# Allocating 640 bytes of small tables ahead of a 52 KB tile ring, in an encoder layer kernel

## The chip, the cores and the metric

The kernel runs on one core of a Trainium2 chip. The metric is device time in microseconds (us), the median of several executions; lower is better. One further execution was taken with the hardware profiler, and every row shown here is from it.

## The reference

One layer of a bidirectional encoder is applied to two batches, 512 tokens ("s") and 256 tokens ("p"), of width 1024, in float32:

```
xn = RMSNorm(x)
[qA|kA|vA|qB|kB|vB] = xn @ w_in                 # w_in: 1024 x 2304
oA = dilated sliding-window attention, 8 heads, three dilations merged
oB = windowed attention (+-128 tokens) with a sink logit, 8 query heads, 2 key heads
h  = x + concat(RMSNorm(oA), RMSNorm(oB)) @ w_o # 1024 x 1024
y  = h + relu(RMSNorm(h) @ w_up)^2 @ w_down     # 1024 x 4096, 4096 x 1024
```

## The kernel before

Float32 products are made from three matmuls: each operand is split into a high part and a low part (both float32r), and high x high, high x low and low x high are summed in PSUM. `mm3(out, xh, xl, wh, wl, ...)` issues the three, on lines 213, 214 and 215; in the projections and in the down product the x part is the stationary operand (loaded with a weight load) and the weight part is the moving operand, 512 columns. `product` with `mm` (lines 682 to 694) does the same for w_up, with the w_up part stationary and 384 columns of x moving. In the profile a matmul is named out<-moving,stationary.

Tiles come from pools. A pool gives each tag its own stretch of each partition, in the order in which the first tile of the tag is asked for; tiles of one tag share its buffers in turn. The pool `sb` lives through the whole kernel, `att` until the attention and both output projections are issued, and `mlp` takes the place of `att` after that. The tag "heap" in `sb`, called the ring here, has `NHEAP = 13` buffers of 4,096 bytes per partition. It holds in turn, among others:

- the raw weights of the first two projections (`wis0_*r`, `wis1_*r`), half of the queries and keys of batch s, the queries and keys of batch p, the transposed x of batch p (`xTp`), most transposed probabilities (`PTs`), the mixed heads of batch p (`mxp`);
- the normalised rows ahead of their transpose (`hs`), the raw and split parts of w_up (`wu..r`, `wu..a`, `wu..b`, `wu..c`, `wu..h`, `wu..l`) and of w_down (`wd..r`, `wd..h`, `wd..l`).

It does not hold: the x of batch s (`xTs`), the values of batch s (`vAs`), the mixed heads of batch s (`mxs`), the activations `u` and the MLP's input `hn`, which lie in the tag "big"; one low part of w_up, `wul`, one block of `hn` and the keys `kBs`, which lie in the tag "b12"; the split weights of the projections (`wis_*`, `wip_*`, `wos_*`, `wop_*`), most of their raw loads, and the probabilities before the transpose (`prs`), which lie in `att`; the four sums `T` and one block `wu..d`, which lie in `mlp`; the identity matrix `ident`, which is the moving operand of every transpose.

These are the addresses in bytes per partition that the program of before is built with. The pool begins behind 4,096 bytes of scratch and four constants of 32 bytes each.

| what | first byte | remainder by 256 |
|---|---|---|
| ring "heap", 13 x 4,096 | 4,224 | 128 |
| `ident`, 512 | 57,472 | 128 |
| `mhalf`, `rx`, `ones`, `gat`, 32 each | 57,984 to 58,111 | 128, 160, 192, 224 |
| tag "big", 5 x 12,288 | 74,496 | 0 |
| tag "b12", 12,288 | 136,384 | 192 |
| split weights in `att`, 6 x 4,096 | 169,472 | 0 |
| raw weights in `att`, 2 x 4,096 | 208,384 | 0 |
| `prs` in `att`, 6 x 2,048 | 216,576 | 0 |
| `T` in `mlp`, 4 x 12,288 | 169,536 | 64 |
| `wu..d` in `mlp` | 206,400 | 64 |

Within a tile, the slices that the matmuls take start at further multiples of 512 bytes, so an operand has the remainder of its tile.

The order of the work is the order of the program text, arranged by the generators `fills`, `pace` and `attend` from written-out costs, and by the tile scheduler; none of it reads an address. The MLP runs as 16 passes over pairs of w_up and w_down blocks. From pass 2 on, `up(i)` makes seven products of 12 matmuls (lines 683; blocks A00, S2, S1, A01, S4, S3, A11) and `down(i)` 72 matmuls (6 token tiles x 2 halves x 2 blocks x 3). `down(i)` is interleaved with `up(i+1)` for its first token tile and runs by itself after that, except for `down(0)` and the last.

Of the kernel before, what the change touches and what calls it, by code (L numbers as in the profile page):

```python
# [8 lines left out]
F32 = mybir.dt.float32  # L9
# [5 lines left out]
P = 128  # L15
# [25 lines left out]
def tile_encoder(ctx: ExitStack, tc: tile.TileContext, a):  # L41
# [5 lines left out]
    sb = ctx.enter_context(tc.tile_pool(name="sb", bufs=1))  # L47
# [5 lines left out]
    def heap(shape, dt, name):  # L53
        return sb.tile(shape, dt, tag="heap", name=name, bufs=NHEAP)
# [6 lines left out]
        return ps.tile([P, 512], F32, tag="ps", name=name, bufs=8)  # L61

    zero = heap([P, 512], mybir.dt.bfloat16, "zero")
    nc.vector.memset(zero, 0.0)
    warm = acc("warm")
    for _ in range(WARM):
        nc.tensor.matmul(warm, zero[:, :P], zero, start=True, stop=True)
    ident = sb.tile([P, P], F32, name="ident")  # L70
    make_identity(nc, ident)
    mhalf = sb.tile([P, 8], F32, name="mhalf")
    nc.gpsimd.memset(mhalf, -0.5)
    rx = sb.tile([P, 6], F32, name="rx")
    ones = sb.tile([P, 1], F32, name="ones")
    nc.vector.memset(ones, 1.0)
    gat = sb.tile([P, 8], F32, name="gat")
    nc.scalar.dma_start(gat, a["gat"])
    nc.scalar.activation(rx[:, 0:1], ones, AF.Exp)

# [956 lines left out]
```

## Time before, and how to read its profile

| | us |
|---|---|
| median of 3 executions | 901.11 (899.32 to 901.6) |
| the profiled execution, its own time | 899.42 |
| its span, first to last instruction | 897.6 |
| TensorE busy in the span | 883.7 |

The profile names engines PE (TensorE matmul), PEld (TensorE weight load), DVE (VectorE), ACT (ScalarE), POOL (GpSimd) and SP (SyncE, which issues DMAs). L215 is line 215 of the kernel. A matmul's listed duration includes its time in the pipeline, so consecutive matmuls overlap in it; the pace of TensorE is read from the distance between the starts of matmuls that follow each other. In the chain of waits a run of pieces of one engine, each starting where the last ended, gives these starts directly.

### The profile page before, as it was taken

Reading aid. Unit: us, or ns where it says so; the run is one execution under the profiler, and the core shown is the slowest. Engines: PE = TensorE matmul, PEld = TensorE weight load, DVE = VectorE, ACT = ScalarE, POOL = GpSimd, SP = SyncE. Lnnn points to the kernel's source line nnn. Section 1 sums busy time; section 2 is a strip of 40 time slices with the busy share of each in tenths; the row PEclk is TensorE's granted clock in tenths of the full one; section 3 lists DMA queues with packets and bytes.
Section 4 is the critical chain, followed back from the end, with each engine's and each line's share of the span. In section 5 each row is a group of like instructions: output and inputs, shape, how many; then the busy total and the mean of one; then the engine's idle time right before and its main releaser. Section 6 shows DMA issues by size and latency. Waiting matters only on the chain.

```text
span 897.6 us, 12569 instructions
## 1 busy us (share of the span) xinstructions
PE 883.7 (98%) x4740; PEld 762.7 (85%) x4740; DVE 627.8 (70%) x1134; ACT 401.7 (45%) x795; POOL 232.2 (26%) x252
## 2 busy tenths in 40 slices
PE   9999999999999999899999999999999999999998
PEld 6877888877878788798889988988998898899886
DVE  7666778887898756959777557657755765775654
ACT  6466578777777644735323222322322232232210
POOL 0412645481254100502511220221122022112000
PEclk9999999999999999999999999999999999999999
DMA  9121111321125115304122112112211211121103
GB/s 367 45 93 49 50 46 48 118 71 63 57 78 188 65 48 191 114 1 141 50 92 94 41 54 94 49 70 71 94 43 53 95 49 68 71 95 42 53 1 140
DMA packets 22252, 72.92 MB, mean 81 GB/s; under 512 B 2480, under 2 KB 2992, under 8 KB 22192
## 3 DMA queue, kind: packets, MB, share of 16 engines
q1 hardware_dynamic: 22048, 72.12, 22.8%
q8 instruction: 37, 0.61, 0.3%
q14 instruction: 23, 0.19, 0.1%
q10 hardware_dynamic: 144, 0.00, 0.0%
HBM read 68.97 MB, written 3.15 MB: 80 GB/s over the span
## 4 chain that ended last, share of the span: by engine, by line
PE 88%; DVE 6%; ACT 3%; issue 1%; DMA 1%; POOL 1%; SPq 0%; ACTq 0%
PE pjs L213 4%; PE pjs L215 4%; PE pjs L214 4%; PE u L683 3%; PE wos L213 2%; PE scsA L425 2%; PE wos L215 2%; PE wos L214 2%; PE pjp L213 2%; PE ptsA L479 1%; PE pjp L215 1%; PE pjp L214 1%; PE posA L497 1%; PE scsB L425 1%; DVE hs L641 1%
## 5 line engine op out<-in xcount | busy, mean ns | idle before, releaser
L798 POOL TENSOR_TENSOR s<-s,s 128x384 f32<-128x384 f32 x14 | 15.0, 1070 | 70.3 <-ACT s L790 70.3
L436 ACT ACTIVATE prsA<-prsA,NM 128x512 f32<-128x512 f32 x32 | 23.1, 724 | 18.1 <-DVE NM L432 18.0
L704 ACT ACTIVATE u<-s 128x384 fp32r<-128x384 f32 x28 | 14.7, 524 | 27.6 <-DVE s L782 26.9
L432 DVE CUSTOM_DVE_ANT_0 prsA<-scsA,MA 128x512 f32<-128x512 f32 x32 | 21.5, 683 | 6.5 <-PE scsA L425 6.4
L704 ACT ACTIVATE u<-r 128x384 fp32r<-128x384 f32 x22 | 11.6, 528 | 31.7 <-DVE r L793 19.4
L432 DVE CUSTOM_DVE_ANT_0 prsB<-scsB,MB,cst 128x256 f32<-128x256 f32 (+1 forms) x32 | 16.8, 542 | 5.4 <-PE scsB L425 3.3
L436 ACT ACTIVATE prsB<-prsB,NM 128x256 f32<-128x256 f32 (+1 forms) x32 | 17.7, 556 | 5.4 <-DVE NM L432 4.0
L479 PE MATMUL ptsA<-ident,prsA 128*128 128x128 f32 x128 | 17.4, 273 | 1.2 <-ACT xTp1h L201 1.2
L213 PE MATMUL pjs<-wis_0hi,xTs 128*128 128x512 f32 (+1 forms) x48 | 17.8, 393 | 0.1
L213 PE MATMUL pjs<-wis_1hi,xTs 128*128 128x512 f32 (+1 forms) x48 | 17.5, 375 | 0.0
L479 PEld LDWEIGHTS ptsA<-ident,prsA 128*128 128x128 f32 x128 | 14.8, 140 | 3.1 <-ACT xTp1h L201 1.4
L214 PE MATMUL pjs<-wis_1lo,xTs 128*128 128x512 f32 (+1 forms) x48 | 17.2, 359 | 0.0
L215 PE MATMUL pjs<-wis_1hi,xTs 128*128 128x512 f32 (+1 forms) x48 | 17.1, 357 | 0.0
L214 PE MATMUL pjs<-wis_0lo,xTs 128*128 128x512 f32 (+1 forms) x48 | 16.6, 356 | 0.0
L215 PE MATMUL pjs<-wis_0hi,xTs 128*128 128x512 f32 (+1 forms) x48 | 16.5, 355 | 0.0
L782 DVE SCALAR_TENSOR_TENSOR s<-s 128x384 f32<-128x384 f32 x28 | 15.4, 551 | 0.0
L705 DVE TENSOR_TENSOR u<-s,u 128x384 fp32r<-128x384 f32 x28 | 15.4, 550 | 0.0
L673 PE MATMUL hT<-ident,hs 128*128 128x128 f32 x96 | 12.2, 273 | 3.1 <-ACT wop_1hi L149 2.3
L673 PEld LDWEIGHTS hT<-ident,hs 128*128 128x128 f32 x96 | 10.9, 140 | 4.4 <-ACT wop_1hi L149 2.7
L705 DVE TENSOR_TENSOR u<-r,u 128x384 fp32r<-128x384 f32 x22 | 13.1, 599 | 1.9 <-ACT u L704 1.8
L213 PEld LDWEIGHTS pjs<-wis_0hi,xTs 128*128 128x128 f32 x48 | 9.4, 199 | 4.1 <-ACT xTs L201 1.0
L215 PE MATMUL pjs<-wis_2hi,xTs 128*128 128x512 f32 x32 | 12.8, 400 | 0.0
(1540 smaller groups left out, 3254.6 us busy)
## 6 DMA issues: line engine op xcount, KB each, us to landing
wis_1r<-w_in SPq DMA_DIRECT2D x5, 512.0 KB, 5.7
wip_0r<-w_in SPq DMA_DIRECT2D x5, 512.0 KB, 3.1
wip_1r<-w_in SPq DMA_DIRECT2D x5, 512.0 KB, 3.2
wis_2r<-w_in SPq DMA_DIRECT2D x4, 512.0 KB, 5.7
wis_3r<-w_in SPq DMA_DIRECT2D x4, 512.0 KB, 6.0
wis_0r<-w_in SPq DMA_DIRECT2D x4, 512.0 KB, 5.8
wip_2r<-w_in SPq DMA_DIRECT2D x4, 512.0 KB, 3.2
wip_3r<-w_in SPq DMA_DIRECT2D x4, 512.0 KB, 3.1
```

What stands on the lines that cost most here:

```text
L213: gated(nc.tensor.matmul(out, xh, wh, start=start, stop=False))
L214: nc.tensor.matmul(out, xh, wl, start=False, stop=False)
L215: nc.tensor.matmul(out, xl, wh, start=False, stop=stop)
L425: last[0] = nc.tensor.matmul(sc[j][:, :w], q[x][pr, qt * P:(qt + 1) * P], k[y][pr, k0 * P:k1 * P], start=(x + y == 0), stop=(x == 1))
L432: nc.vector.tensor_tensor_reduce(tt[:, :w], sc[j][:, :w], mask(qt, k0, w), scale=1.0, scalar=BIG if sink is None else sink[:, h - 8:h - 7] ...
L436: nc.scalar.activation(tt[:, :w], tt[:, :w], AF.Exp, bias=nm_ap, scale=-1.0, accum_out=LS[:, b.t0 + qt, h:h + 1])
L479: last[0] = nc.tensor.transpose(pt[:, n * P:(n + 1) * P], tts[j][:, n * P:(n + 1) * P], ident)
L673: tr = nc.tensor.transpose(pt[:, i * P:(i + 1) * P], hs[:, i * P:(i + 1) * P], ident)
L683: i = nc.tensor.matmul(out, w, x, start=start, stop=stop, skip_group_check=True)
L704: nc.scalar.activation(u[:, 0, us], r, AF.Copy)
L705: nc.vector.tensor_sub(u[:, 1, us], r, u[:, 0, us].bitcast(F32))
L782: nc.vector.scalar_tensor_tensor(c, c, 0.0, c, op0=ALU.max, op1=ALU.mult)
```

## The change

The five `sb.tile` calls of the small tables `ident`, `mhalf`, `rx`, `ones` and `gat` are moved up, ahead of the first tile of the ring. No instruction is added, removed or moved.

```
+    ident = sb.tile([P, P], F32, name="ident")
+    mhalf = sb.tile([P, 8], F32, name="mhalf")
+    rx = sb.tile([P, 6], F32, name="rx")
+    ones = sb.tile([P, 1], F32, name="ones")
+    gat = sb.tile([P, 8], F32, name="gat")
 
     zero = heap([P, 512], mybir.dt.bfloat16, "zero")
     nc.vector.memset(zero, 0.0)
     warm = acc("warm")
     for _ in range(WARM):
         nc.tensor.matmul(warm, zero[:, :P], zero, start=True, stop=True)
-    ident = sb.tile([P, P], F32, name="ident")
     make_identity(nc, ident)
-    mhalf = sb.tile([P, 8], F32, name="mhalf")
     nc.gpsimd.memset(mhalf, -0.5)
-    rx = sb.tile([P, 6], F32, name="rx")
-    ones = sb.tile([P, 1], F32, name="ones")
     nc.vector.memset(ones, 1.0)
-    gat = sb.tile([P, 8], F32, name="gat")
     nc.scalar.dma_start(gat, a["gat"])
     nc.scalar.activation(rx[:, 0:1], ones, AF.Exp)
```

The tables take 512 + 4 x 32 = 640 bytes.

## Rows read from the trace of the kernel before

**Rows 1.** Page: busy time and share of each engine; PE and clock in 40 slices

```profile
PE 883.7 (98%) x4740; PEld 762.7 (85%) x4740; DVE 627.8 (70%) x1134; ACT 401.7 (45%) x795; POOL 232.2 (26%) x252
...
PE   9999999999999999899999999999999999999998
...
PEclk9999999999999999999999999999999999999999
```

**Rows 2.** Busy time by stretch: window, length, engines with instructions, clock, DMA share, GB/s

```profile
0.00:25.00 25.00, 23.72 (x94) 17.70 (x95) 18.73 (x32) 16.75 (x21) 0.92 (x9) 1.00 0.93 368
...
150.00:300.00 150.00, 144.62 (x934) 119.27 (x933) 125.89 (x308) 114.00 (x290) 63.59 (x84) 0.99 0.26 89
300.00:450.00 150.00, 146.06 (x813) 127.86 (x812) 111.66 (x189) 74.44 (x150) 39.33 (x35) 1.00 0.26 91
450.00:540.00 90.00, 90.00 (x449) 80.89 (x448) 58.60 (x88) 26.87 (x38) 17.71 (x15) 1.00 0.19 66
...
700.00:800.00 100.00, 100.00 (x500) 90.21 (x499) 66.01 (x99) 28.92 (x42) 18.37 (x15) 1.00 0.20 69
```

**Rows 3.** Chain of waits, 580 to 600 us: start, length, what (62 pieces of `down(5)`)

```profile
580.35 0.23 PE y5s L214
580.57 0.23 PE y5s L215
...
581.96 0.24 PE y5s L215
...
583.59 0.24 PE y5s L213
...
585.21 0.24 PE y5s L214
...
594.51 0.23 PE y5p L215
594.74 2.11 PE u7a L683 x12
```

**Rows 4.** Chain of waits, 9 to 28 us: the first projection, 24 matmuls between rows

```profile
11.31 0.91 PE pjs L213 x4
...
16.75 0.91 PE pjs L213 x4
...
22.19 0.91 PE pjs L213 x4
...
27.63 0.45 PE xss L240 x5
```

**Rows 5.** Chain of waits, 336 to 350 us: output projection of batch s

```profile
339.46 0.23 PE wos L215
...
341.55 0.23 PE wos L215
...
346.32 0.23 PE wos L215
346.55 0.44 PE mxp L592 x4
```

**Rows 6.** TensorE in order of time, 349.5 to 366 us: output projection of batch p

```profile
349.77 0.39 PE L214 MATMUL wop<-wop_0lo,mxp 128*128 128x512 f32 x1
...
357.90 0.63 PE L213 MATMUL wop<-wop_3hi,mxp 128*128 128x512 f32 x2
...
363.25 0.40 PE L215 MATMUL wop<-wop_0hi,mxp 128*128 128x512 f32 x1
365.96 0.30 PE L673 MATMUL hT<-ident,hs 128*128 128x128 f32 x1 [2.31 <-ACT wop_1hi L149]
```

**Rows 7.** Chain of waits, 379 to 401 us: first w_up products, both w_up parts in the ring

```profile
379.35 12.50 PE u L683 x71
391.85 1.75 PE hT L673 x16
```

**Rows 8.** Chain of waits, 500 to 518 us: the products of `up(4)`

```profile
500.48 2.11 PE u4a L683 x12
502.59 2.09 PE u4b L683 x12
504.68 2.09 PE u4c L683 x12
506.77 2.12 PE u4a L683 x12
508.88 2.09 PE u4b L683 x12
...
511.91 2.12 PE u4c L683 x12
...
515.40 2.11 PE u4b L683 x12
```

**Rows 9.** Chain of waits, 84 to 90 us: 256 columns, moving in the ring

```profile
85.97 1.90 PE posA L497 x16
```

**Rows 10.** Chain of waits, 137 to 142.5 us: 256 columns, no operand in the ring

```profile
137.24 0.12 PE pjs L214
...
139.16 0.12 PE pjs L215
```

**Rows 11.** Groups by shape: splits of 1024-column weights on ACT and DVE

```profile
L149 ACT ACTIVATE wos_3hi<-wos_3r 128x1024 fp32r<-128x1024 f32 x2 | 2.1, 1062 | 1.4 <-PE wos L215 1.4
...
L149 ACT ACTIVATE wd10h<-wd10r 128x1024 fp32r<-128x1024 f32 x1 | 1.1, 1062 | 0.1
...
L153 DVE TENSOR_TENSOR wos_0lo<-wos_0r,wos_0hi 128x1024 fp32r<-128x1024 f32 x2 | 2.5, 1226 | 2.6 <-ACT wos_0hi L149 2.1 <-PE ptpA L469 0.5
...
L153 DVE TENSOR_TENSOR wd12l<-wd12r,wd12h 128x1024 fp32r<-128x1024 f32 x1 | 1.2, 1226 | 0.2 <-ACT wd12h L149 0.2
```

**Rows 12.** DMA issues: size of one, median us from issue to landing

```profile
wos_1r<-w_o SPq DMA_DIRECT2D x2, 512.0 KB, 3.2
...
wd22r<-w_down SPq DMA_DIRECT2D x1, 512.0 KB, 3.2
```

**Rows 13.** Groups by shape: transposes

```profile
L479 PE MATMUL ptsA<-ident,prsA 128*128 128x128 f32 x128 | 17.4, 273 | 1.2 <-ACT xTp1h L201 1.2
...
L673 PE MATMUL hT<-ident,hs 128*128 128x128 f32 x96 | 12.2, 273 | 3.1 <-ACT wop_1hi L149 2.3 <-DVE hs L666 0.5 <-DVE hs L665 0.3
```

**Rows 14.** Groups of the first 12 us: the first split

```profile
L151 DVE CAST wis_0hi<-wis_0r 128x512 fp32r<-128x512 f32 x1 | 0.4, 426 | 3.2 <-DMA wis_0r<-w_in 3.2
```

## The prediction

> **What bounds the kernel now.** I read the page first: TensorE is busy 98% of the span, its clock row shows the full level (2.4 GHz) in every slice, VectorE is at 70% [rows 1]. Then the stretches: from 450 us on TensorE is busy 100% of each window while no other engine passes 66%, and even the two attention and output-projection stretches are at 96 and 97% [rows 2]. So time can only be won or lost in how fast TensorE steps from one matmul to the next, and in the MLP each nanosecond of that step is a nanosecond of the result. The chain of waits shows the step, because its pieces follow each other start to start.
>
> **The step depends on where the operands lie.** Take five runs of 512-column matmuls, all at the full clock.
>
> - First projection, moving in `att` (remainder 0 by 256), stationary in "big" (0): 27.63 - 11.31 = 16.32 us for 72 matmuls, 226.7 ns each [rows 4].
> - Output projection of batch s, same two places: after other work the first nine take 341.55 - 339.46 = 2.09 us, 232 ns each, then 21 take 346.32 - 341.55 = 4.77 us, 227 ns each [rows 5].
> - Output projection of batch p, same code and the same buffers for the moving operand, stationary in the ring (128): 357.90 - 349.77 = 8.13 us for 35, 232.3 ns each, and it never settles [rows 6].
> - Down product, moving in the ring (128), stationary in "big" (0): 594.74 - 580.35 = 14.39 us for 62, 232.1 ns each; every seventh step is a 0.24 (581.96, 583.59, 585.21), to the end of the run [rows 3].
>
> So a run whose two operands have the same remainder settles, after some nine matmuls, at 226.7 ns; one whose remainders differ by 128 stays at 232.1 to 232.3. Two of the runs differ from the others only in which operand is the odd one. The excess is 5.4 ns, 2.4%.
>
> **What the change does, part by part.** It issues nothing new and moves no instruction; the tables keep the same 640 bytes. The ring moves up by 640 bytes, from 4,224 to 4,864 = 19 x 256, remainder 0; all that lies behind the tables stays; `ident` goes to 4,224, which is again remainder 128.
>
> 1. *Down product.* 16 passes x 72 = 1,152 matmuls; moving goes from 128 to 0, stationary stays at 0, the pair of the first projection. In the 14 interleaved passes a run of 62 is unbroken [rows 3]; less nine to settle, 53 x 5.4 ns = 0.286 us, x 14 = 4.0 us. The two other passes: 63 x 5.4 ns x 2 = 0.7 us. The ten matmuls of a pass that stand between products I leave at 232 ns. Gain 4.7 us; bounds 0 and 1,152 x 5.4 ns = 6.2 us.
> 2. *First w_up products.* 192 matmuls of 384 columns, three quarters of them with `hn` in "big" (0) and both w_up parts in the ring: 12.50 us for 71, 176.1 ns [rows 7]. No row has this shape settled; between 226.7 ns at 512 columns and 16 steps in 139.16 - 137.24 = 1.92 us, 120.0 ns, at 256 [rows 10], the line gives 173.3 ns, an estimate. The long run gives 62 x 2.8 ns = 0.17 us, the short ones as much again in all. Gain 0.3 us; bounds 0 and 0.5.
> 3. *Products of `up`.* With `hn`: 14 x 36 = 504, at 2.11 or 2.12 us for 12, 176.4 ns; with `T` and a ring block: 504, at 2.09 for 12, 174.2 ns [rows 8]. Each third weight load is `wul` at 192, which stays. For `hn` the ring loads then agree and `wul` does not: between 173.3 and 176.4 ns, so 0 to 1.6 us gained. For `T` (64) the differences from its loads go from 192 and 128 to 64 and 128, which are those that `hn` has now at 176.4 ns: 0 to 1.1 us lost. I take half of each: they nearly cancel, 0.
> 4. *Projections of batch p.* 192 matmuls with `xTp` and 96 with `mxp` as stationary would agree. The first kind comes in short runs between attention steps, too short to settle; after the run of the second kind TensorE idles 2.31 us for a weight split [rows 6], which takes up what it wins. 0; bound 288 x 5.5 ns = 1.6 us gained.
> 5. *Probabilities times values.* 128 matmuls of 256 columns with `PTs` as moving operand and "big" as stationary, some 190 with those of the other kinds: 1.90 us for 16, 118.8 ns [rows 9], against 120.0 where both agree [rows 10]. At this width agreeing is the slower: loss 190 x 1.2 ns = 0.2 us.
> 6. *Transposes.* `ident` and `hs` agree before (128 and 128) and not after; `prs` (0) does not agree before. Both last 273 ns [rows 13]: 0.
> 7. *Other engines.* The split of a 1,024-column weight takes 1,062 ns on ScalarE and 1,226 on VectorE whether its tiles are at 0 (`wos`) or at 128 (`wd`) [rows 11]: 0. Were it not, both lie beside TensorE's full stretches.
> 8. *Loads.* 512 KB land in 3.2 us at 0 and at 128 [rows 12]: 0. The one load waited for at the start costs 3.2 us of VectorE [rows 14]. The Trainium skill (DMA: Bandwidth & Descriptors, How a descriptor splits into AXI transactions) says that a descriptor off a 256-byte boundary starts at the boundary below and pays for the unused beats; for a 4,096-byte row at 128 that is 132 beats for 128, an estimate, 3% of a load. The two landing times here show none of it, and by the rule the start would win 0.1 us.
>
> Sum: -4.7 - 0.3 + 0.2 = -4.8 us. The profiled execution took 899.42 us, 897.6 of span and 1.8 around it that the change does not touch: it would take 894.6. It lies 1.7 us below the median of the three; on the median, 901.1 - 4.8 = 896.3 us, 0.5% less. A measurement of this kernel can tell 0.3%, 2.7 us, from no change.
>
> **Rivals.**
>
> *The remainder is not the cause (no change).* The operands of the slow runs lie in the ring, at low addresses, and those of the fast runs do not; the place, or something else in which those runs differ, could set the step, and the ring stays where it is but for 640 bytes. Against it: the nine slow steps ahead of the settled ones in the same run [rows 5] look like two streams that fall into step, which a place alone would not give. Then 901.1 us, within 0.3%. The Trainium skill speaks for this rival: TensorE: Matmul & The Clock Gate, Part 2: What happens when you issue a matmul, gives TensorE two independent SBUF read ports, one for the streamed operand and one for the weights, so that their addresses could not matter. The two paces of one shape at one clock, 226.7 and 232.1 ns, do not agree with that being all.
>
> *Every pair that agrees gains at once.* No nine to settle, the short runs too: the upper bounds of 1, 3 and 4 without the loss for `T`: 6.2 + 0.5 + 1.6 + 1.6 = 9.9 us, 891.2. Against it: rows 5 show the slow start.
>
> *Slower: agreeing too well.* By 512, `att` has remainder 0 and "big" 256, and so do the settled runs; the moved ring has 256, the same as "big". A pair equal by 512 stands in the trace only as `wu..d` with `T` (64 and 64): 2.11 us for 12, the last piece of the group, against 2.09 for the other `T` products, 1.7 ns more each [rows 8]. If the down product did likewise instead of settling, it would lose 1,152 x 1.7 ns = 1.9 us; if each step were as its slowest now, 0.24 us, 9.1 us. I take the middle: 1,152 x 4 ns = 4.6 us, 905.7. It decides once the down step passes 232.1 + 2.3 = 234.4 ns. Against it: that group is cut by a change of neighbours, which alone slows the first nine.
>
> **How the numbers follow.** Forecast 0.66, with its own range of 894.3 to 898.4 (the down product between the settled gain and half of it); no change 0.18; gains at once 0.09; slower 0.07. The time given is the forecast's, 896.3. The range takes in the no-change case up to the highest of the runs shown and some of the larger gain: 892.5 to 901.7. Faster by over 0.3%: the forecast and the larger gain, less a little for a half-sized gain, 0.74; within 0.3%: 0.19; slower: 0.07.
>
> **What would show it.** In the profile after: the run of 62 down matmuls takes about 9 x 232 + 53 x 226.7 ns = 14.1 us instead of 14.39, with no 0.24 behind its ninth; the 71 first w_up products 12.3 instead of 12.50; three passes, 500.48 to 594.74 before (94.3 us), take 93.4. Step 5 shows as 16 `posA` in 1.92, step 6 as 273 ns unchanged, steps 7 and 8 as the same 1,062, 1,226 and 3.2. The prediction is wrong if the down run keeps its seven-step pattern, or settles at a pace other than 226.7, or if `T` products rise above 176.4.

## The result and the profile after

The changed kernel took 892.76 us (median of 4, 892.65 to 894.54) beside 900.84 of the kernel before (4 runs, 899.32 to 901.6): ratio 0.9917, interval 0.9899 to 0.9935. Timed again in five rounds it took 893.67 (6 runs, 892.79 to 894.86) beside 900.42 (11 runs, 899.12 to 904.7): ratio 0.9923, interval 0.9904 to 0.9943. By the medians that is 8.1 us less at first and 6.75 the second time, and the interval of the second leaves 5.1 to 8.6; 4.8 were forecast. The 6.75 us are used below. Of the two profiled executions, 892.82 and 899.42 us, the difference is 6.6.

The page after: the same instructions, shares within a point and the same clock row as in [rows 1]. TensorE's busy time falls from 883.7 to 877.5 us, and GpSimd's from 232.2 to 229.1.

```profile
span 891.0 us, 12569 instructions
...
PE 877.5 (98%) x4740; PEld 761.9 (86%) x4740; DVE 628.6 (71%) x1134; ACT 402.0 (45%) x795; POOL 229.1 (26%) x252
...
PEclk9999999999999999999999999999999999999999
```

By stretch, the columns being those of [rows 2]: TensorE was full in both MLP windows before and is full now, so its busy time can show nothing there. What changes is how many matmuls fit: 456 for 449, and 503 for 500. The windows cut the passes at other places than before, and a pass mixes two widths, so the sign of these counts says more than their size.

```profile
450.00:540.00 90.00, 90.00 (x456) 81.89 (x455) 59.49 (x88) 27.36 (x39) 18.30 (x15) 1.00 0.20 69
700.00:800.00 100.00, 100.00 (x503) 90.64 (x502) 67.10 (x101) 29.96 (x43) 18.30 (x15) 1.00 0.21 73
```

The chain of waits after, in the run of 62 down matmuls that answers to [rows 3]:

```profile
578.21 0.23 PE y5s L214
...
579.81 0.23 PE y5s L215
...
592.28 2.09 PE u7a L683 x12
```

592.28 - 578.21 = 14.07 us, 226.9 ns each, against 14.39 and 232.1 before. The first seven take 579.81 - 578.21 = 1.60 us, 0.01 more than seven steps of 226.7 ns: room for two or three slow ones. The other 55 take 12.47, 226.7 each. No piece of the run has 0.24, where before every seventh had. The three passes from the first product of `up(4)` (below) to that of `up(7)` take 592.28 - 499.28 = 93.0 us, where 93.4 were forecast for 94.3.

The same view for the first w_up products [rows 7], for the products of `up(4)` [rows 8], and for 16 `posA` [rows 9]:

```profile
379.49 12.33 PE u L683 x71
```

```profile
499.28 2.09 PE u4a L683 x12
501.37 2.10 PE u4b L683 x12
503.46 2.11 PE u4c L683 x12
505.57 2.10 PE u4a L683 x12
507.67 2.08 PE u4b L683 x12
...
510.67 2.08 PE u4c L683 x12
...
514.13 2.08 PE u4b L683 x12
```

```profile
85.97 1.91 PE posA L497 x16
```

The seven pieces add up to 14.64 us for 84 matmuls, against 14.73 before. One pass, from the first product of `up(3)` to that of `up(4)`, takes 499.28 - 468.28 = 31.00 us, before 500.48 - 469.06 = 31.42: 0.32 of the 0.42 us come from the down run and 0.09 from the products. The starts of `up(2)` and `up(3)`, before and after:

```profile
437.68 2.11 PE u2a L683 x12
...
469.06 2.11 PE u3a L683 x12
```

```profile
437.25 2.09 PE u2a L683 x12
...
468.28 2.09 PE u3a L683 x12
```

**Where the time went.** The chain over the whole span is cut at the first product of `up(2)`, the start of the steady MLP. It starts at 437.25 us after and at 437.68 before. From there to the end of the span it is 891.0 - 437.25 = 453.75 us after and 897.6 - 437.68 = 459.9 before. So the attention stretches and the first pass give 0.4 us, and the steady MLP 6.15. Fourteen passes at 0.42 us are about 5.9 of it; the rest comes behind the last full pass.

### The profile page after: what moved, and what is told of

The parts are those of the page before. It is cut to its first block, busy times and chain, and to the rows that moved or that the text cites. A ratio compares the mean times of both kernels' runs of the same rounds, so it can differ in the third digit from the quotient of the medians.

```text
span 891.0 us, 12569 instructions
## 1 busy us (share of the span) xinstructions
PE 877.5 (98%) x4740; PEld 761.9 (86%) x4740; DVE 628.6 (71%) x1134; ACT 402.0 (45%) x795; POOL 229.1 (26%) x252
## 4 chain that ended last, share of the span: by engine, by line
PE 89%; DVE 4%; ACT 4%; issue 2%; DMA 1%; POOL 0%; SPq 0%; ACTq 0%
PE pjs L213 4%; PE pjs L214 4%; PE pjs L215 3%; PE u L683 3%; PE wos L213 2%; PE scsA L425 2%; PE wos L215 2%; PE wos L214 2%; PE pjp L213 1%; PE ptsA L479 1%; PE pjp L215 1%; PE pjp L214 1%; PE hT L673 1%; PE posA L497 1%; PE scsB L425 1%
## 5 line engine op out<-in xcount | busy, mean ns | idle before, releaser
L214 PE MATMUL pjs<-wis_3lo,xTs 128*128 128x512 f32 x32 | 12.7, 396 | 0.0
```

The lines of the kernel that those rows point to most:

```text
L214: nc.tensor.matmul(out, xh, wl, start=False, stop=False)
```

## The experiments

Three theories were told apart. **D**: the step depends on the *difference* of the byte addresses of moving and stationary operand, taken by 256. **A**: each operand on its own must begin at a multiple of 256. **P**: the place counts, that is, the ring's position or its distance from the other tiles, whatever the remainder. In every variant of the layer below, all instructions stand in the same order on every engine; only addresses differ.

**The step by itself (`steps`, `steps2`).** A kernel that leaves out the whole layer and runs 60 float32r matmuls per pair of addresses, with the weight tiles and moving tiles alternating as in the down product. Its time is not to be compared with that of the layer.

```
for m, s, n in CASES:   # bytes added to the moving, to the stationary operand; columns
    pt = ps.tile([P, 512], F32, tag="ps", name=f"m{m}s{s}n{n}x", bufs=8)
    for i in range(60):
        x = mv[:, (i % 3 == 1) * 2048 + m // 4:][:, :n]
        w = wt[:, (i % 6 // 3 * 2 + (i % 3 == 2)) * 1024 + s // 4:][:, :P]
        nc.tensor.matmul(pt[:, :n], w, x, start=i == 0, stop=i == 59)
    ...
```

> This kernel computes nothing of the layer: it runs 60 matmuls of the down product's form for each pair of remainders (of moving and stationary operand, in bytes, both tiles at multiples of 512) and width, and its steps are read from the chain of waits. Theory D (the difference of the two remainders by 256 decides): at 512 columns (0,0), (128,128), (64,64), (0,256), (256,0) and (256,256) settle at 226.7 ns a step; (0,128) and (128,0) stay at 232.1; (0,64), (64,0), (0,192), (0,32), (0,16) do not settle and lie between 227 and 236. At 384 columns (0,0) and (64,64) take 173.3 ns, (0,128) about 176; at 256 columns (0,0) takes 120.0 and (0,128) 118.7. Theory A (an operand is read at full pace only from a multiple of 256): (128,128) and (64,64) are as slow as (0,128) or slower. Theory P (the place of the ring, not the remainder): all 512-column cases have one pace. The rival of an equal remainder by 512: (0,0) and (256,256) slower than (0,256).

The chain of waits of `steps` gives one piece for each pair (m: moving, s: stationary, n: columns); a piece divided by 60 is the step.

```profile
14.10 15.47 PE m0s0n512x L42 x60
29.57 13.60 PE m128s128n512x L42 x60
43.18 13.61 PE m64s64n512x L42 x60
56.79 13.94 PE m0s128n512x L42 x60
70.73 13.94 PE m128s0n512x L42 x60
84.67 14.00 PE m0s64n512x L42 x60
...
112.67 13.74 PE m0s192n512x L42 x60
...
154.41 13.60 PE m0s256n512x L42 x60
...
181.61 13.60 PE m256s256n512x L42 x60
195.21 10.43 PE m0s0n384x L42 x60
205.63 10.56 PE m0s128n384x L42 x60
216.20 10.60 PE m0s64n384x L42 x60
226.79 10.40 PE m64s0n384x L42 x60
...
258.00 7.19 PE m0s0n256x L42 x60
265.19 7.12 PE m0s128n256x L42 x60
272.30 6.82 PE m0s64n256x L42 x60
```

The first pair, 0 and 0, begins while TensorE is still slow: its first starts lie 0.43 us apart, and the whole piece takes 15.47 us. Its pace is read from its end. The same view from 24 us on has its last 25 matmuls, 226.8 ns each:

```profile
23.90 5.67 PE m0s0n512x L42 x25
```

What to see: equal remainders give 226.7 ns at 0 (the end of the first piece, and [rows 4]), at 64 and at 128 alike (13.60 us), so A falls. A difference of 128 gives 13.94, 232.3 ns, whichever operand is the odd one. These are the two paces of the layer. Equal by 512 or apart by 256 makes no difference (13.60), so the rival "agreeing too well" has nothing behind it. At 384 columns a moving operand 64 bytes ahead of the stationary one costs nothing (10.40 against 10.43), one 64 behind costs 2.8 ns (10.60). At 256 columns the order turns round: equal remainders are the slowest, 119.8 ns, then 128 with 118.7, and a moving operand 64 behind is the fastest, 113.7.

**Undone in part and done another way.** `rest_at_128` takes the kernel before and, in place of moving the ring, moves everything behind the tables by 128 bytes, so that the ring stays at remainder 128 and the rest joins it there:

```
     gat = sb.tile([P, 8], F32, name="gat")
+    sb.tile([P, 32], F32, name="pad")
```

> The kernel before, with the ring where it was (4,224, remainder 128) and 128 unused bytes behind gat, so that everything behind the tables moves by 128 instead: big 128, att 128, b12 64, T 192. Each difference between ring, big, att, b12 and T is as after the change, and hardly any operand is at a multiple of 256. Theory D: as after the change, 892.8 us, ratio to before 0.991. Theory A: the first projections and the output projection of batch s become slow too, 576 matmuls x 5 ns: 903 us, ratio 1.003. Theory P: 901 us, ratio 1.000.

`ring_at_128` takes the changed kernel, with the tables ahead of the ring, and puts the ring back at remainder 128, leaving the rest where it was:

```
+    sb.tile([P, 32], F32, name="pada")   # behind gat, ahead of the ring
     ...
+    sb.tile([P, 32], F32, name="padb")   # behind the ring's first tile
     warm = acc("warm")
```

> The kernel after the change, tables first, with 128 unused bytes ahead of the ring and 128 behind it: the ring begins at 4,992, remainder 128 again, and all behind it keeps its remainder by 256. Theories D and A: as before the change, 900.8 us, ratio 1.000. Theory P (the new place of the tables or of the ring is the gain): 893 us, ratio 0.991.

`all_at_0` takes the changed kernel and brings the tiles that still had another remainder (`T` and `wu..d` among them) to 0 too, with three unused tiles of 64, 128 and 64 bytes:

```
+    sb.tile([P, 16], F32, name="pada")   # ahead of b.kv
+    sb.tile([P, 32], F32, name="padb")   # behind it
+    att.tile([P, 16], F32, name="padc")  # behind LS
```

> The kernel after the change, with 64 unused bytes ahead of the tag b12, 128 behind it and 64 in att, so that b12, T and wu..d begin at remainder 0 too, as ring, big and the split weights do. Theories D and A: the 1,008 products of up and part of the first w_up products settle at 173.3 ns instead of 172 to 176.6 (mean 174.3): 1.0 to 1.5 us less than after the change, 891.4 us, ratio to before 0.9897. Theory P: as after the change, ratio 0.991.

The changed kernel itself ran again in the same rounds as the next one:

> The kernel after the change once more, in five rounds, beside the next. Theory D, by the steps that were measured (226.7 ns instead of 232.1 in the down product, products of up 1.0 us, first w_up products 0.3 us less, against 0.2 lost): 6.5 to 7 us less than before, ratio 0.992 to 0.993. If the 8.1 us between the two medians were all of it and the profiled pair's 6.6 us too little: ratio 0.991.

`big_at_128` takes the kernel before and moves the "big" tiles to 128, with the raw x and the sums of batch s that lie just ahead of them, and nothing else to another remainder, so that the down product agrees while `att` and "big", which agreed in the projections, no longer do:

```
     gat = sb.tile([P, 8], F32, name="gat")
+    sb.tile([P, 32], F32, name="pada")
     ...
+    if b is S_: sb.tile([P, 32], F32, name="padb")   # x_stats, ahead of tmp
```

> The kernel before, with the ring where it was (remainder 128) and big moved from remainder 0 to 128 by 128 unused bytes; 128 more bytes behind big keep all else at its remainder. Theory D: the down product now agrees (128, 128) and wins 5.5 us, the first w_up products (hn in big, ring) 0.3; the first projections and the output projection of batch s (split weights at 0, big at 128) lose where they were settled, some 340 and 60 matmuls, 1.2 and 0.4 us; posA loses 0.1; together 4.1 us less, 896.3 us, ratio 0.9955. In its trace the 72 matmuls of the first projection that took 16.32 us take 16.72, the 62 of the down product 14.06 instead of 14.39. Theory A (full pace only from multiples of 256): nothing wins and the projections lose, 902.5 us, ratio 1.002.

Measured (medians, with the kernel before in the same call; "MLP" is the profiled span from the first product of `up(2)` on, "down" the step in the run of 62):

| kernel | ring, "big" | us | before | ratio, interval | MLP us | down ns |
|---|---|---|---|---|---|---|
| before | 128, 0 | | 900.39, 900.42 | | 459.9 | 232.1 |
| after | 0, 0 | 892.76 | 900.84 | 0.9917, 0.9899 to 0.9935 | 453.75 | 226.9 |
| after, again | 0, 0 | 893.67 | 900.42 | 0.9923, 0.9904 to 0.9943 | 453.8 | 226.9 |
| `rest_at_128` | 128, 128 | 893.96 | 900.39 | 0.9931, 0.9917 to 0.9946 | 453.8 | 226.8 |
| `ring_at_128` | 128, 0 | 900.66 | 900.39 | 1.0005, 0.9995 to 1.0014 | 459.9 | 232.3 |
| `all_at_0` | 0, 0 | 892.8 | 900.39 | 0.9923, 0.9905 to 0.994 | 453.8 | 227.3 |
| `big_at_128` | 128, 128 | 896.01 | 900.42 | 0.9942, 0.9923 to 0.9961 | 453.9 | 226.8 |

`ring_at_128` has the order of allocation of the changed kernel and none of its gain, and `rest_at_128` has the ring exactly where it was and the whole gain: P falls, and A a second time. The run of 62 in the chain of waits of these two, `ring_at_128` first:

```profile
581.27 0.23 PE y5s L216
...
595.67 2.11 PE u7a L685 x12
```

```profile
581.91 0.23 PE y5s L215
...
595.97 2.09 PE u7a L684 x12
```

14.40 us in the first, 14.06 in the second. `big_at_128` pulls the two ends of D apart in one kernel: its down run falls into the fast step, and its first projection leaves it. The chain of waits there, 24 matmuls between the first and second of these rows, as in [rows 4]:

```profile
17.64 0.92 PE pjs L214 x4
...
23.22 0.93 PE pjs L214 x4
```

5.58 us, 232.5 ns each, where [rows 4] has 5.44 for 24. Its gain is 4.4 us by the medians, 2.3 less than that of the changed kernel. Its MLP is as short as that of the changed kernel, so the 2.3 lie ahead of it; what they are made of stands at the end of the next section.

`all_at_0` gains nothing more, where 1.0 to 1.5 us were expected. Its products are faster, seven pieces of 2.08 to 2.10 us that add up to 14.58, 0.06 less than after, but the pass is as long, 31.00 us (499.64 - 468.64): its down run takes 14.09 us for 14.07, and the rest lies in the matmuls of the pass that stand between products.

**The rule's extent (`steps2`).** The same loop with more differences, and with bfloat16 tiles (b for r in the names).

> As the kernel of steps, computing nothing of the layer, with other pairs. Theory D in its strict form (only the difference moving minus stationary by 256 counts): at 512 columns (0,s) and (256-s,0) have the same pace, for each s, and (192,64), (64,192) that of (128,0), 232.3 ns; 0 and 256 give 226.7, the rest lie between. The run of steps gave (0,192) 229.0 but (64,0) 233.2, which the strict form does not allow; if the difference counts by 512 instead, (0,320) is not (0,64), and (64,0) goes with (0,448), not with (0,192). For bfloat16 operands: if the effect is that of 4-byte operands, all pairs have one pace at each width; if it is of the addresses, (0,128) differs from (0,0) at 512 columns here too.

```profile
29.80 13.99 PE rm0s32n512x L49 x60
...
71.83 13.94 PE rm0s128n512x L49 x60
...
99.77 13.75 PE rm0s192n512x L49 x60
...
155.12 13.74 PE rm64s0n512x L49 x60
...
182.87 14.00 PE rm128s0n512x L49 x60
196.87 14.05 PE rm160s0n512x L49 x60
...
301.84 12.96 PE bm0s0n512x L49 x60
...
327.76 12.95 PE bm0s128n512x L49 x60
```

By difference, moving less stationary: 0 gives 226.7 ns, +64 (0 and 192, or 64 and 0) 229.0, 128 from 232.3 to 233.3, and the other multiples of 32 between 233.2 and 234.2. So the strict form of D, one pace for each difference, does not hold: 128 and 0 took 13.94 us in `steps` and 14.00 here, and 64 and 0 took 13.99 there and 13.74 here. Only equal remainders gave one pace wherever they stood. In bfloat16 the address changes nothing: 215.9 ns each.

## Why the forecast held, and where its sizes were off

The mechanism is the one forecast: 512-column matmuls whose operands agree in their remainder by 256 fall into a step of 226.7 ns, and the 62 down matmuls did so. The experiments show it from four sides (ring moved, rest moved, "big" alone moved, ring moved back) and in a kernel with nothing else in it. Why the hardware has this rule is not shown by any run. The rule that was weighed in the rival, two independent read ports (the Trainium skill, TensorE: Matmul & The Clock Gate, Part 2), holds here for bfloat16 only, as far as the step tells: in float32r the two addresses matter together.

The size was off by 1.95 us, 6.75 for 4.8. Two terms of the sum carry most of it.

- **Part 1, the settling.** Nine slow steps were taken from [rows 5], where the run stands behind other work. In the steady MLP it stands behind products of `up`, and two or three were enough: 0.32 us a pass for 0.286, which over 14 passes is 4.5 for 4.0. By the forecast's own sign, "no 0.24 behind its ninth", there is none at all. In that the run comes near the rival in which every pair gains at once. `all_at_0`, which has the same addresses in this run and takes 0.02 us longer for it, shows that the settling depends on what ran ahead, and no run here shows how.
- **Part 3, the products of `up`.** Taken as 0, they gain 0.09 us a pass, 1.3 in all. Going by the names of the operands, the first, fourth and sixth of the seven pieces are those of `hn`; the second, third and fifth those of `T` with a ring block, and the last is `T` with `wu..d`. The `hn` pieces went from 6.35 to 6.27 us, 1.1 over 14 passes where 0.8 was taken. The `T` pieces with a ring block went from 6.27 to 6.29, so the feared loss came, 0.3 where 0.55 was taken. The term left out is the last piece: neither `T` nor `wu..d` changed its remainder, so the sum had nothing for it, and it went from 2.11 to 2.08, 0.4 over 14 passes. Its cause lies outside its own two operands. The rows round each piece to 0.01 us, so these sums are good to some 0.2.

The cost of a difference read from a loop of one pair does not carry over to these pieces, in which every third weight load is at another remainder. By `steps` and `steps2` at 384 columns a difference of 128 takes 176.0 ns a step, +64 173.3 and -64 176.7. Two ring loads and one `wul` in three would make 175.1 for `hn` before and 176.5 for `T` before; [rows 8] have 176.4 and 174.2. Why is not shown.

The others: part 2 forecast 0.3 and the 71 products went from 12.50 to 12.33, 0.17, as its long run was worked out. Part 4 is 0 as forecast: the 71 products behind it start at 379.49 us, before at 379.35, with the lower clock told of below in between. Part 5 has the right sign, 1.91 us for 1.90, and `steps` confirms that agreeing is slower at 256 columns (119.8 against 118.7 for 128), but by less than the forecast's total can show. Part 6, the transposes: those of `prs` still take 273 ns, and those of `hs` have this row after.

```profile
L673 PE MATMUL hT<-ident,hs 128*128 128x128 f32 x96 | 13.5, 292 | 3.1 <-ACT wop_1hi L149 2.3
```

They rise from a mean of 273 to 292 ns, against the forecast, but the addresses are not the cause. `all_at_0` has the same pair of remainders and 273:

```profile
L673 PE MATMUL hT<-ident,hs 128*128 128x128 f32 x96 | 12.2, 273 | 3.4 <-ACT wop_1hi L149 2.6 <-DVE hs L666 0.5 <-DVE hs L665 0.3
```

What differs is the granted clock. These transposes begin at 365.73 us after, behind a wait of 2.3 us for the split of `wop_1`, and there the clock falls to its lower level, 1.2 GHz, for 3.4 us; the digits of the page are too coarse to show it. The busy time by stretch from 365.8 to 369.1 us has it as 0.50 after and as 1.00 in `all_at_0`, as it was before behind the same wait:

```profile
365.80:369.10 3.30, 3.30 (x14) 3.00 (x15) 2.86 (x6) 1.91 (x3) 2.71 (x2) 0.50 0.18 38
```

```profile
365.80:369.10 3.30, 2.60 (x20) 2.45 (x21) 3.30 (x6) 3.14 (x6) 1.94 (x1) 1.00 0.06 19
```

Why it fell in the one and held in the other is not shown. It fell there in the second profile of the changed kernel too.

Parts 7 and 8 came as forecast. The split of `wd10` on ScalarE takes 1,065 ns after, that of `wd12` on VectorE 1,226 [rows 11], and the DMA issues after have, for [rows 12]:

```profile
wd22r<-w_down SPq DMA_DIRECT2D x1, 512.0 KB, 3.2
```

A load into a remainder of 0 still lands in 3.2 us, as one into 128 did, and so does the median load of w_down in both. The 3% that were estimated from the Trainium skill (DMA: Bandwidth & Descriptors, How a descriptor splits into AXI transactions) are not to be seen in this kernel; they would be 0.1 us of such a load, which is all that this view can tell apart.

Two slips in the prediction's working bear on no conclusion. The "five runs" of 512 columns that it lists are four. And the middle of 1.7 and 7.9 ns, in the rival of agreeing too well, is 4.8 and not 4 ns, so that its price would be 5.5 us, 906.6.

**What lies ahead of the MLP in two variants.** The profiled executions of `rest_at_128` and `big_at_128` reach the first product of `up(2)` at 440.94 and 440.67 us, 3 us later than the kernel before. For `rest_at_128` D expects 0.4 less and for `big_at_128` 1.6 more. The traces show two places where it arises.

- The first projection of batch p begins at 152.3 us before and in `rest_at_128`, and at 154.2 in `big_at_128`: 1.9 us that are near D's 1.6 for the projections.
- From the first `scsB` to the first `scpA` matmul, the windowed attention, it is 69.5 us before, 71.0 in both `big_at_128` and `ring_at_128`, and 73.6 in `rest_at_128`. `ring_at_128` has every remainder of the kernel before, so 1.5 us come and go without them.

What differs there is again the granted clock. Each of the four has a stretch at the lower level, 3.4 us long, in `rest_at_128` 6.8 with another 3.4 at 226 us. Before, it begins at 194 us and ends ahead of a wait for VectorE; in the variants it begins between 202 and 205, in the last moments of that wait or behind it. The wait, before and in `ring_at_128`:

```profile
202.74 0.36 PE L497 MATMUL posB<-PTsB_00h,kBs 128*128 128x256 f32 x1 [0.94 <-DVE PTsB L482]
```

```profile
202.36 0.53 PE L499 MATMUL posB<-PTsB_00h,kBs 128*128 128x256 f32 x1 [2.21 <-DVE PTsB L484]
```

It is 2.21 us long in all three variants and 0.94 before. So before, TensorE lost its time where it would have waited anyway, and in the variants where it would not. The mean clock of `rest_at_128` from 185 to 255 us is 0.93, that of the other three 0.98. So the 3 us are no evidence against D: in `big_at_128` 1.9 of them are the projections, and the rest goes with the place and the length of the slow stretch. What makes the clock fall at one place or the other is open, and with it whether the addresses have a part in that.

## What to carry to other kernels

Where TensorE is the bound and the operands are float32r, give the moving and the stationary operand of the long 512-column runs the same byte remainder by 256; a few unused bytes do it, and here they were worth 2.4% of each such step and 0.8% of the kernel. It is the difference that counts, so either operand can be moved, but any move also changes the pairs that agreed before: list all pairs, as `big_at_128` shows, and with their widths, since at 256 columns agreeing was the slowest. Look for it in the distances between starts in the chain of waits, since neither the busy share nor the clock shows it.

## What the runs showed that was not expected

- The rule is not one of alignment: 64 and 64, or 128 and 128, are as fast as 0 and 0 (13.60 us for 60).
- The difference has a sign: moving 64 bytes ahead of stationary costs 2.3 ns of a step of 512 columns (13.74 us) in three of four runs, 64 behind 6.7 (14.00).
- At 256 columns equal remainders are the slowest of the three pairs tried, 119.8 ns against 113.7 for 0 and 64, 5%. Each was run once.
- One pair can have two paces: 64 and 0 took 13.99 us for 60 in `steps`, behind a run of 0 and 64, and 13.74 in `steps2`, behind a run of 32 and 0; 128 and 0 took 13.94 and 14.00.
- A piece whose operands both stayed where they were (`T` with `wu..d`) got faster, from 2.11 to 2.08 us for 12.
- The clock fell for 3.4 us in some executions and not in others at the same place in the work, behind the same wait.
